# A hybrid encoder step on one core: in-place convolutions, spread row statistics, and queue positions for the next norm and the next mixer

## The chip, the cores and the metric

The kernel runs on one core of a Trainium2 chip. The metric is the device time of one execution in microseconds (us), as the median of several runs. A core has five engines that work side by side and meet only at semaphores: TensorE (PE) multiplies matrices out of SBUF into PSUM, VectorE (DVE), ScalarE (ACT) and GpSimd (POOL) work element by element, and SyncE (SP) here only issues DMA transfers. Each engine takes its instructions in one fixed order, so an instruction that waits holds everything queued behind it on the same engine. PSUM is small: a tile in it is free again only when the last instruction that reads it has ended.

## The reference

One step of one layer of a streaming encoder, in float32, over 1024 prompt tokens (one new stream) and 32 sample tokens (one running stream with carried states):

```python
h = mixer(rms_norm(x, g_mix_pre), ...)            # in-projection, three recurrences, out-projection
x = x + rms_norm(h, g_mix_post)
h = conv_ffn(rms_norm(x, g_ffn_pre), ...)         # up, causal convolution, gelu(gate)*val, down
x = x + rms_norm(h, g_ffn_post)
```

`mixer` projects each token's 1024 values with `w_in` to the inputs of three groups of heads:

- GLA, 6 heads (key width 32, value width 64): q, k, v, a low-rank gate that gives log-decays, and an output gate.
- HGRN2, 5 heads (64, 64): `q = silu(hq) / 8`, `k` and the log-decay from a sigmoid of one projection, and v.
- mLSTM, 5 heads (64, 64): q and k go through a causal convolution of width 4 and silu, and there are v, an input gate, a forget gate and an output gate. Its convolution's last three rows are returned as a cache, for the prompt and for the sample.

GLA and HGRN2 run S_t = diag(a_t) S_{t-1} + k_t v_t^T and o_t = S_t^T q_t; mLSTM runs a stabilised matrix memory with a running maximum m and a normaliser n. Each head's output is normalised (`x * rsqrt(mean(x*x) + 1e-6)`), multiplied by a gain and a gate, and the heads' outputs side by side (`cat`, 1024 wide) go through `w_out`. All final states are outputs.

## The kernel before

**Numbers and products.** A float32 product is made of three matmuls of the type fp32r: each operand is split into a high and a low part, and `mm3` (L99 to L102) adds high x high, high x low and low x high in PSUM. So each weight tile is loaded (`r`), its high part copied by ACT or DVE and its low part subtracted by POOL or DVE (`split`, L104 to L109). Group 0 stores the low parts to DRAM and groups 1 and 2 load them again (`weights`, `kept`).

**Groups.** The tokens come in units of 128 (u = 0 to 7; unit 8 is the 32 sample tokens) and the in-projection in three groups: units 0 to 2, units 3 to 5, and units 6, 7 and 8 (`GROUPS`, L27). For each group `inproj` (L352) is a generator whose steps are, in this order:

1. The norm. `scale_x` (L291) loads x of a unit, squares and sums it on ACT (L300), forms the reciprocal root on POOL (`rstd_of`, L216 to L219) and scales x on DVE (L303). `norm_group` (L306) turns the scaled x over on PE (xt, L314) and copies out high parts (ACT, xh L316) and low parts (DVE, xl L317). Between them the first token-major block, `vg(0)`.
2. Feature tiles, `feat(t)`: 128 output features by all tokens of the group, 24 matmuls each into one PSUM tile `pf` of the tag "big", which has three banks for everything that the projections make. Their order is 8 (a convolution), 6, 7, 3 (decays), 2, 0 (k and q of GLA), 4, 5, 1 (q of HGRN2, `silu_q` L529), 10 to 13 (convolutions). `silu_q` forms tanh(x/2) on ACT, scales it in place on DVE (L532: 0.0625 th + 0.0625) and multiplies it with the PSUM tile on DVE (L533); the factor 1/16 holds the 1/8 of the reference and the 1/2 of silu from tanh. `decay` and `decays` (L493 to L521) form the log-decays and their running sums. Results go to DRAM (`out_units`), where the mixer picks them up by unit.
3. A convolution, `conv(j, ps)` (L367 to L395): ACT copies the PSUM tile to `pc` (L372), POOL puts the three halo columns ahead and saves the new ones (L373, L374; `halo`), in group 2 the sample's columns and cache (`mcache`) go in and the caches are stored, two DMAs for each of five tiles (L378, L379). ACT forms y = pc * w3 + bias (L382), DVE adds three taps to y (L384), ACT takes its tanh, and DVE writes the product to a further tile `mo` (L389), which is stored. y has one buffer.
4. The mLSTM's row statistics, `rows()` (L541 to L600): running sums and maxima along five rows, then three tiny products of the decays (dcp, L590) copied to `dcs` (L592), and for each unit a transpose of the rows `r_st` (L596) copied to `cols` (L598). These small PSUM tiles come from a pool `psm` under a tag that the mixers use too (named mi in the profile). The generator is started after feature tile 3 and finished in one go after feature tile 1 (`next(row, None)`).
5. The token-major blocks 1 to 7 of 256 features: v and the output gates. `vg_store` (L408) copies v out on ACT (L412), or forms a gate from a tanh on ACT and one or two DVE operations. In group 2 `vg_across` makes them feature-major and turns them back (vf L456, pb L444). In block 5 of groups 0 and 1 the next group's `scale_x` is run. The loads of x for the next group are written there too.

**Mixers beside them.** `mixer(u, g, ci0)` (L700 to L965) is a generator for one unit, with two chunks of 64 tokens, in 17 steps. It loads `qkb` (q, k and the summed log-decays b; L703), mqk, v and gates in one step; forms eb = exp(b) on ACT (L743), dec and qz = q * eb on DVE; kh = exp(b_last - b) * k (DVE L758, ACT, DVE), turned over on PE and copied to kt (L767); six levels of decayed scores (sc, then P); the outputs og and oh and the states S (L857, L858); `finish` (L883 to L892: square on ACT, sum on DVE, reciprocal root, two products); then the mLSTM part with sm, kw, C, oi and om, and a last `finish`. `cat` goes to DRAM. The eight prompt mixers and the sample's one run beside what follows: those of group 0 beside the in-projection of group 1, and so on. `merge` (L1429) and `pump` take so many steps of the mixers for each step of the main generator. The last group's mixers run beside the out-projection, whose order of units is 0, 1, 2, 3, 8, 4, 5, then 6 and 7.

**Out-projection.** `outproj` (L994 to L1093) turns cat over (ctp, L1016), copies high and low halves out (ch L1019 on ACT, cl L1020 on DVE), multiplies with `w_out` (zp), squares and copies z, normalises it with the residual (L1060, L1061), forms the FFN's norm and turns it over for the FFN (fxt). The FFN, some half of the time, follows.

**What sets the order.** The program is written with a tile framework that puts the instructions of each engine in order by priority (the order in which the program issues them) along a simulated timeline. `tc.high_priority(offset=100)` moves instructions ahead by so many places; the small PE operations of the mixer go through it (`first`). `tc.issue_after(ins)` puts an instruction behind another one in the queue of the same engine.

Of the kernel before, what the change touches and what calls it, by code (L numbers as in the profile page):

```python
# [8 lines left out]
F32 = mybir.dt.float32  # L9
# [4 lines left out]
ALU = mybir.AluOpType  # L14
# [76 lines left out]
def body(ctx: ExitStack, tc: tile.TileContext, a: dict):  # L91
# [19 lines left out]
    def tanh(out, in_, scale):  # L111
        act.activation(out, in_, AF.Tanh, scale=scale)

# [101 lines left out]

    def rstd_of(out, ss, n, cols, width):  # L216

        pool.tensor_scalar(out, ss, 1.0 / width, EPS, op0=ALU.mult, op1=ALU.add)  # L218
        pool.tensor_tensor(out, out, mhalf[:n, :cols], op=ALU.pow)  # L219
# [68 lines left out]

    xn_of = {}

    def scale_x(g):  # L291
        for (u, off, n) in units_of(g):
            x = x_in.pop(u, None)
            x = load_x(u) if x is None else x
            if g == 0:
                jk = mx.tile([128, 1024], BF16, tag=("gt", "cat", "qkb")[u], name=f"jk{u}", bufs=1)
            else:
                jk = p1.tile([128, 1024], BF16, tag="jk", name=f"jk{u}", bufs=1)
            ss = p1.tile([128, 1], F32, tag="ss", name=f"ss{u}", bufs=2)
            act.activation(jk[:n], x[:n], AF.Square, accum_out=ss[:n])  # L300
            rs = p1.tile([128, 1], F32, tag="rs", name=f"rs{u}", bufs=2)
            rstd_of(rs[:n], ss[:n], n, 1, 1024)
            dve.scalar_tensor_tensor(x[:n], x[:n], rs[:n], gx[:n], op0=ALU.mult, op1=ALU.mult)  # L303
            xn_of[u] = x
            yield
# [46 lines left out]
    def inproj(g, xh, xl, normed, scaled=None):  # L352
# [16 lines left out]
        def conv(j, ps):  # L369
            W = 3 + pl + (3 + sl if sl else 0)  # L370
            pc = t1("pc", 2, W)
            act.copy(pc[:, 3:3 + pl], ps[:, :pl])  # L372
            pool.tensor_copy(pc[:, 0:3], halo[:, j, :])  # L373
            pool.tensor_copy(halo[:, j, :], pc[:, pl:pl + 3])  # L374
            if sl:
                act.copy(pc[:, pl + 6:pl + 6 + sl], ps[:, pl:T])
                pool.tensor_copy(pc[:, pl + 3:pl + 6], mcache[:, j, :])
                sp.dma_start(a["q_mc"][:, j, :], pc[:, W - 3:W])  # L378
                sp.dma_start(a["p_mc"][:, j, :], pc[:, pl:pl + 3])  # L379
            L = W - 3  # L380
            y = t1("y", 1, L)
            act.activation(y, pc[:, 3:], AF.Identity, scale=mconv[:, j, 3:4], bias=mconv[:, j, 4:5])  # L382
# [6 lines left out]
            ins = dve.scalar_tensor_tensor(o, th[:, :L], 1.0, y, op0=ALU.add, op1=ALU.mult)  # L389
            if j < 4:  # L390
                out_units(g, mqk_d, mqks_d, ((0, 1, 3, 4)[j], slice(None)), o, pl + 3)
            else:
                for slot, r0 in ((2, 0), (5, 64)):
                    out_units(g, mqk_d, mqks_d, (slot, slice(None)), o, pl + 3, slice(r0, r0 + 64), slice(0, 64))
            return ins  # L395
# [12 lines left out]
        def vg_store(blk, u, off, n, ps):  # L408
            o = mx.tile([128, 256], F32, tag="vg", name=f"vg{u}_{blk}", bufs=3)
            t = t0 + off  # L410
            if blk < 4:
                act.copy(o[:n], ps[:n, :256])  # L412
                sp.dma_start(v_d[t:t + n, 256 * blk:256 * blk + 256], o[:n])
                return
            c0 = 256 * (blk - 4)
            th = mx.tile([128, 256], F32, tag="vth", name=f"vth{u}_{blk}", bufs=1)
            tanh(th[:n], ps[:n, :256], 0.5)
            ns = min(max(704 - c0, 0), 256)
            if ns:
                dve.scalar_tensor_tensor(th[:n, :ns], th[:n, :ns], 1.0, ps[:n, :ns], op0=ALU.add, op1=ALU.mult)  # L420
            if ns < 256:
                dve.tensor_scalar(th[:n, ns:], th[:n, ns:], 1.0, None, op0=ALU.add)
            pool.tensor_tensor(o[:n], th[:n], gh[:n, c0:c0 + 256], op=ALU.mult)
            sp.dma_start(g_d[t:t + n, c0:c0 + 256], o[:n])
# [103 lines left out]

        def silu_q(q, ps, r0):  # L529
            th = t1("th", 1, T + 3)[:, :T]  # L530
            tanh(th[r0:], ps[r0:, :T], 0.5)
            dve.tensor_scalar(th[r0:], th[r0:], 0.0625, 0.0625, op0=ALU.mult, op1=ALU.add)  # L532
            return dve.tensor_tensor(q[r0:], th[r0:], ps[r0:, :T], op=ALU.mult)  # L533

# [6 lines left out]
        def rows():  # L541
# [51 lines left out]
            dcs_of[g] = dcs  # L593
            for (u, off, n) in units_of(g):
                pt = small(128)
                pe.transpose(pt[:n, :], st[:, off:off + n], ident)  # L596
                cl = mx.tile([128, 128], F32, tag="cols", name=f"cols{u}", bufs=6)
                act.copy(cl[:n], pt[:n])  # L598
                cols_of[u] = cl
# [81 lines left out]

    halves, kwi = [], [None]
    def spread(eng, dst, fn, n, half=None):
# [10 lines left out]
    def mixer(u, g, ci0):  # L694
# [47 lines left out]
        ebf = eb[:, :4 * n]  # L742
        act.activation(ebf, b4.rearrange("p f n -> p (f n)"), AF.Exp)  # L743
        eb4 = ebf.rearrange("p (f n) -> p f n", n=n)
# [3 lines left out]
        with ExitStack() as behind:  # L748
            if halves:

                for ins in (kwi[0], halves[1]):
# [5 lines left out]
        b5 = b4.rearrange("p f (k c) -> p (f k) c", c=cl)  # L757
        dve.tensor_tensor(khf.rearrange("p (m c) -> p m c", c=cl), b5[:, :, cl - 1:cl].broadcast_to([128, 4 * nch, cl]),  # L758
                          b5, op=ALU.subtract)
        act.activation(khf, khf, AF.Exp)  # L760
# [121 lines left out]

        def finish(o3, c0, h0, nh):  # L883
# [3 lines left out]
            act.activation(sq3, o3, AF.Square)  # L887
            dve.tensor_reduce(ss[:n, h0:h0 + nh], sq3, axis=mybir.AxisListType.X, op=ALU.add)  # L888
            rstd_of(rs[:n, h0:h0 + nh], ss[:n, h0:h0 + nh], n, nh, 64)
            dve.tensor_tensor(cat[:n, c0:c0 + 64 * nh].rearrange("p (h d) -> p h d", d=64), o3,  # L890
                              rs[:n, h0:h0 + nh].unsqueeze(2).broadcast_to([n, nh, 64]), op=ALU.mult)
            pool.tensor_tensor(cat[:n, c0:c0 + 64 * nh], cat[:n, c0:c0 + 64 * nh], gt[:n, c0:c0 + 64 * nh], op=ALU.mult)  # L892

        finish(og[:n], 0, 0, 6)
        finish(oh[:n], 384, 6, 5)

# [95 lines left out]
    def outproj(p2, W, u):  # L992
# [13 lines left out]
        for hf in range(2):  # L1006
# [7 lines left out]
            for k in range(4):  # L1014
# [3 lines left out]
            cl = p2.tile([128, 4, 128], F32R, tag="cl", name=f"cl{u}{hf}", bufs=3)  # L1018
            ins = (act.copy(ch[:, :, :n], ps[:, :, :n]),  # L1019
                   dve.tensor_tensor(cl[:, :, :n], ps[:, :, :n], ch[:, :, :n].bitcast(F32), op=ALU.subtract))  # L1020
            if u == RING[0]:
# [664 lines left out]
```

## Time and profile before

| | |
|---|---|
| runs | 1427.78, 1431.09 and 1431.6 us; median 1431.09 us |
| profiled execution | 1433.42 us, of which the trace's span is 1431.6 us |
| mean granted clock of PE | 0.983 |
| in-projection of group 0 | from the start to about 157 us |
| groups 1 and 2, with the mixers of the group before | to about 354 and 531 us |
| out-projection with the mixers of group 2 | to about 700 us |
| FFN | to the end |

The profile is one execution with each engine's instructions. Its page gives busy time by engine, the span in slices, the chain of work that ended last, and the costliest groups of instructions. The stage limits in the table are read from the timeline by the names of the tiles. The trace behind the page answers closer questions, and the prediction quotes four kinds of answer:

- Waits: engine, tile and line of the instruction that waited, what released it, and then total wait in us, number and longest.
- Stretches of time: limits and length, then busy us (and instructions) of PE, PE's weight loads, DVE, ACT and POOL, then the granted clock as a share of full speed, the DMA engines' mean busy share and GB/s.
- A timeline: start in us, duration in us, engine, line, operation, out<-in, shapes, and in brackets the idle time of the engine just before with what ended it.
- DMA groups: out<-in, queue, number, KB of one, and the median us from issue to landing.

### The profile page before, as it was taken

The page shows a single profiled execution, that of the slowest core. Times are in us where ns is not written, and L with a number is a line of the kernel's source. Part 1 is how long each engine was busy: PE and PEld are TensorE (multiplying, and loading weights), DVE is VectorE, ACT ScalarE, POOL GpSimd, SP SyncE. Part 2 cuts the span into 40 slices and gives each one's busy share as a digit, 9 for nine tenths or more (in the row PEclk, how much of TensorE's full clock was granted, in tenths as well). Part 3 has the DMA queues.
Part 4 walks back from the last instruction along what each step waited for, and adds up shares of the span by engine and source line. Part 5 has one row for each costly group of instructions (what it writes and reads, how often), then busy time and mean ns, then how long its engine had stood idle before and what let it go on. Part 6 is the DMA issues. An engine that isn't in the chain of part 4 may idle for free.

```text
span 1431.6 us, 30048 instructions
## 1 busy us (share of the span) xinstructions
PE 1375.1 (96%) x11804; PEld 1258.5 (88%) x11804; DVE 1006.9 (70%) x1827; ACT 710.2 (50%) x1403; POOL 273.5 (19%) x456
## 2 busy tenths in 40 slices
PE   7989999999998999899989999999999999999998
PEld 6989889898887887767789999999999999988886
DVE  5796468846597669685888887887888875653644
ACT  5545456535474546243665454554555455543432
POOL 6531111213021244132221111111111110000100
PEclk9999999999999999999999999999999999999999
DMA  9599778766789845352412222222222257775752
GB/s 345 189 317 355 229 244 298 236 228 210 262 248 303 313 124 188 122 178 60 162 54 91 85 82 91 75 78 73 91 75 75 76 183 235 227 230 180 238 180 99
DMA packets 132438, 255.11 MB, mean 178 GB/s; under 512 B 28648, under 2 KB 79368, under 8 KB 132296
## 3 DMA queue, kind: packets, MB, share of 16 engines
q1 hardware_dynamic: 132295, 253.19, 53.3%
q8 instruction: 92, 1.51, 0.4%
q14 instruction: 51, 0.41, 0.1%
HBM read 192.26 MB, written 60.89 MB: 177 GB/s over the span
## 4 chain that ended last, share of the span: by engine, by line
PE 71%; DVE 11%; DMA 8%; ACT 5%; issue 3%; POOL 2%; SPq 1%; DVEq 0%; POOLq 0%; ACTq 0%
PE pd L102 6%; PE pd L101 6%; PE pd L100 6%; PE pux L102 4%; PE pux L100 4%; PE pux L101 4%; PE pv L102 3%; PE pv L100 3%; PE pv L101 3%; PE puw L100 3%; PE puw L101 3%; PE puw L102 3%; DMA qkb<-qkb_d 2%; PE zp L100 2%; PE zp L101 2%
## 5 line engine op out<-in xcount | busy, mean ns | idle before, releaser
L1260 DVE SCALAR_TENSOR_TENSOR y<-uu,fconv_sb,y 128x1060 f32<-128x1060 f32 x88 | 116.3, 1321 | 28.3 <-ACT y L1258 27.5
L102 PE MATMUL pd<-wd,hl 128*128 128x512 f32 x264 | 105.1, 399 | 0.0
L101 PE MATMUL pd<-wd,hh 128*128 128x512 f32 x264 | 104.2, 395 | 0.0
L100 PE MATMUL pd<-wd,hh 128*128 128x512 f32 x264 | 103.5, 393 | 0.0
L1254 POOL COPY uu<-uu 128x2 f32<-128x2 f32 x44 | 35.3, 802 | 210.0 <-DVE uu L1202 209.9
L1197 ACT COPY c<-pux 128x274 f32<-128x274 f32 (+1 forms) x132 | 48.9, 375 | 41.2 <-PE pux L102 38.3
L1258 ACT ACTIVATE y<-uu,fconv_sb 128x1060 f32<-128x1060 f32 x44 | 56.0, 1273 | 21.1 <-POOL uu L1255 20.6
L100 PE MATMUL zp<-woh,ch 128*128 128x512 f32 (+1 forms) x144 | 58.8, 415 | 3.9 <-DVE cl L1020 2.9
L101 PEld LDWEIGHTS pd<-wd,hh 128*128 128x128 f32 x264 | 49.6, 188 | 12.5
L100 PEld LDWEIGHTS pd<-wd,hh 128*128 128x128 f32 x264 | 49.6, 188 | 11.7
L102 PEld LDWEIGHTS pd<-wd,hl 128*128 128x128 f32 x264 | 49.6, 188 | 11.4
L100 PE MATMUL pv<-wt_0h,xh 128*128 128x256 f32 (+2 forms) x195 | 57.8, 297 | 1.7 <-ACT xh L316 1.7
L101 PE MATMUL zp<-wol,ch 128*128 128x512 f32 (+1 forms) x144 | 58.8, 408 | 0.0
L102 PE MATMUL zp<-woh,cl 128*128 128x512 f32 (+1 forms) x144 | 58.2, 408 | 0.2 <-DVE cl L1020 0.2
L102 PE MATMUL pv<-wt_1h,xl 128*128 128x256 f32 (+2 forms) x195 | 57.4, 294 | 0.5 <-DVE xl L317 0.5
L102 PE MATMUL pv<-wt_0h,xl 128*128 128x256 f32 (+2 forms) x195 | 57.1, 293 | 0.6 <-DVE xl L317 0.6
L101 PE MATMUL pv<-wt_1l,xh 128*128 128x256 f32 (+2 forms) x195 | 56.9, 292 | 0.0
L100 PE MATMUL pv<-wt_1h,xh 128*128 128x256 f32 (+2 forms) x195 | 56.9, 292 | 0.0
L101 PE MATMUL pv<-wt_0l,xh 128*128 128x256 f32 (+2 forms) x195 | 56.8, 291 | 0.1
L100 PE MATMUL pd<-hh,wd 128*128 128x288 f32 x176 | 52.1, 297 | 0.0
L101 PE MATMUL pd<-hl,wd 128*128 128x288 f32 x176 | 52.1, 296 | 0.0
L218 POOL TENSOR_SCALAR hrs<-hss 128x5 f32<-128x5 f32 (+3 forms) x27 | 14.5, 537 | 196.4 <-DVE hss L888 195.8
(1675 smaller groups left out, 5179.5 us busy)
## 6 DMA issues: line engine op xcount, KB each, us to landing
h_d<-y SPq DMA_DIRECT2D x22, 530.0 KB, 3.3
wt_0r<-in_w_tok SPq DMA_DIRECT2D x21, 512.0 KB, 5.5
wt_1r<-in_w_tok SPq DMA_DIRECT2D x21, 512.0 KB, 5.9
wt_0l<-lt_d SPq DMA_DIRECT2D x14, 512.0 KB, 4.5
wt_1l<-lt_d SPq DMA_DIRECT2D x14, 512.0 KB, 5.6
qkb<-qkb_d SPq DMA_DIRECT2D x8, 768.0 KB, 6.4
hr<-h_d SPq DMA_DIRECT2D x44, 128.0 KB, 3.3
hr<-h_d SPq DMA_DIRECT2D x22, 192.0 KB, 4.1
```

Of the source, the lines that this page charges most:

```text
L100: pe.matmul(ps, lh[0], rh[0], start=first, stop=False, **kw)
L101: pe.matmul(ps, lh[0], rh[1], start=False, stop=False, **kw)
L102: return pe.matmul(ps, lh[1], rh[0], start=False, stop=last, **kw)
L218: pool.tensor_scalar(out, ss, 1.0 / width, EPS, op0=ALU.mult, op1=ALU.add)
L1197: kept[name] = act.copy(t, ps)
L1254: pool.tensor_copy(u[:, GAP_P:GAP_P + 2], u[:, GAP_S - 2:GAP_S])
L1258: act.activation(y, u, AF.Identity, scale=fconv[:, j, 2:3], bias=fconv[:, j, 3:4])
L1260: dve.scalar_tensor_tensor(y, uu[i][:, s:s + NCOL], fconv[:, j, s:s + 1], y, op0=ALU.mult, op1=ALU.add)
```

## The change

It touches the in-projections, the mixers' beginnings and two copies of the out-projection. No matmul is added or removed, and the FFN is as it was.

1. `silu_q` is one DVE operation, (th + 1) * ps. HGRN2's q is thereby 16 times larger; `finish` for its heads takes 16 * 16 * 1e-6 in place of 1e-6 (`by=16.0`), so that the norm gives the same.
2. `conv` works in place: y has three buffers, the product is written to y, and `mo` is gone. In group 2 the caches are gathered in `mcache` and `halo` (one more small POOL copy for each of five tiles) and stored once, two DMAs in place of ten.
3. `rows()` gives up control before the small products and before each transpose, and is taken up after each of the four last convolution tiles. In group 0 the transposes go to a PSUM tile of their own (`rows0`, under the tag "o").
4. `scale_x` of groups 1 and 2: the square is put behind ACT's last tanh of `vg_store` and the scaling behind DVE's last gate operation (`vgi`). The loads of x are issued in block 2.
5. `mixer`: qkb is loaded in two DMAs, b first. The exponential eb is put behind the previous mixer's second square of `finish` on ACT, and kh's subtraction behind the previous mixer's last addition to S on DVE (`outs`).
6. `outproj`: the copies ch and cl are issued at a priority 100 places ahead.

```diff
@@ scale_x
-            act.activation(jk[:n], x[:n], AF.Square, accum_out=ss[:n])
+            with tc.issue_after(vgi[0].ins) if vgi else ExitStack():
+                act.activation(jk[:n], x[:n], AF.Square, accum_out=ss[:n])
             rs = p1.tile([128, 1], F32, tag="rs", name=f"rs{u}", bufs=2)
             rstd_of(rs[:n], ss[:n], n, 1, 1024)
-            dve.scalar_tensor_tensor(x[:n], x[:n], rs[:n], gx[:n], op0=ALU.mult, op1=ALU.mult)
+            with tc.issue_after(vgi[1].ins) if vgi else ExitStack():
+                dve.scalar_tensor_tensor(x[:n], x[:n], rs[:n], gx[:n], op0=ALU.mult, op1=ALU.mult)
@@ conv
-                sp.dma_start(a["q_mc"][:, j, :], pc[:, W - 3:W])
-                sp.dma_start(a["p_mc"][:, j, :], pc[:, pl:pl + 3])
+                pool.tensor_copy(mcache[:, j, :], pc[:, W - 3:W])
+                if j == 3:
+                    sp.dma_start(a["q_mc"], mcache)
+                    sp.dma_start(a["p_mc"], halo)
             L = W - 3
-            y = t1("y", 1, L)
+            y = t1("y", 3, L)
...
-            o = t1("mo", 2, L)
-            ins = dve.scalar_tensor_tensor(o, th[:, :L], 1.0, y, op0=ALU.add, op1=ALU.mult)
+            ins = dve.scalar_tensor_tensor(y, th[:, :L], 1.0, y, op0=ALU.add, op1=ALU.mult)
...
@@ vg_store
-            tanh(th[:n], ps[:n, :256], 0.5)
+            ia = tanh(th[:n], ps[:n, :256], 0.5)
...
+            vgi[:] = ia, iv
@@ silu_q
-            dve.tensor_scalar(th[r0:], th[r0:], 0.0625, 0.0625, op0=ALU.mult, op1=ALU.add)
-            return dve.tensor_tensor(q[r0:], th[r0:], ps[r0:, :T], op=ALU.mult)
+            return dve.scalar_tensor_tensor(q[r0:], th[r0:], 1.0, ps[r0:, :T], op0=ALU.add, op1=ALU.mult)
@@ rows
             yield
+
+            own = psm.tile([128, 3, 128], F32, tag="o", name="rows0", bufs=2) if g == 0 else None
             dcp = small(3, 8)
...
-            for (u, off, n) in units_of(g):
-                pt = small(128)
+            for i, (u, off, n) in enumerate(units_of(g)):
+                yield
+                pt = small(128) if own is None else own[:, i]
                 pe.transpose(pt[:n, :], st[:, off:off + n], ident)
@@ inproj
         decays(2, ins)
-
-        next(row, None)
         yield
         for t, j in ((10, 0), (11, 1), (12, 2), (13, 3)):
             ins = conv(j, feat(t))
             if j == 0:
                 decays(3, ins)
+
+            next(row, None)
             yield
...
             yield from vg(blk)
+            if blk == 2 and g < 2:
+                for (u, off, n) in units_of(g + 1):
+                    x_in[u] = load_x(u)
@@ mixer
-        sp.dma_start(qkb[:, :12 * n], (qkb_d[u] if u < 8 else qkbs_d).rearrange("p a f n -> p (a f n)"))
+        for s0, s1 in ((2, 3), (0, 2)):
+            sp.dma_start(qkb[:, 4 * n * s0:4 * n * s1],
+                         (qkb_d[u] if u < 8 else qkbs_d)[:, s0:s1].rearrange("p a f n -> p (a f n)"))
...
-        act.activation(ebf, b4.rearrange("p f n -> p (f n)"), AF.Exp)
+        with tc.issue_after(outs[0].ins) if outs else ExitStack():
+            act.activation(ebf, b4.rearrange("p f n -> p (f n)"), AF.Exp)
...
+        with tc.issue_after(outs[1].ins) if outs else ExitStack():
+            dve.tensor_tensor(khf.rearrange("p (m c) -> p m c", c=cl), b5[:, :, cl - 1:cl].broadcast_to([128, 4 * nch, cl]),
+                              b5, op=ALU.subtract)
...
-            dve.tensor_tensor(Sn, Sn, up, op=ALU.add)
+            si = dve.tensor_tensor(Sn, Sn, up, op=ALU.add)
...
+        outs[:] = finish(oh[:n], 384, 6, 5, 16.0), si
@@ outproj
-            ins = (act.copy(ch[:, :, :n], ps[:, :, :n]),
-                   dve.tensor_tensor(cl[:, :, :n], ps[:, :, :n], ch[:, :, :n].bitcast(F32), op=ALU.subtract))
+            with tc.high_priority(offset=AHEAD):
+                ins = (act.copy(ch[:, :, :n], ps[:, :, :n]),
+                       dve.tensor_tensor(cl[:, :, :n], ps[:, :, :n], ch[:, :, :n].bitcast(F32), op=ALU.subtract))
```

More of the change, by code (lines that the diff above doesn't have):

```diff
@@ L111, in tanh @@
     def tanh(out, in_, scale):
-        act.activation(out, in_, AF.Tanh, scale=scale)
+        return act.activation(out, in_, AF.Tanh, scale=scale)
     dr = ctx.enter_context(tc.tile_pool(name="dr", bufs=1, space=DRAM))
@@ L214, in body, with rstd_of @@
     dve.tensor_scalar(oml, lb, -1.0, 1.0, op0=ALU.mult, op1=ALU.add)
-    def rstd_of(out, ss, n, cols, width):
-        pool.tensor_scalar(out, ss, 1.0 / width, EPS, op0=ALU.mult, op1=ALU.add)
+    def rstd_of(out, ss, n, cols, width, eps=EPS):
+        pool.tensor_scalar(out, ss, 1.0 / width, eps, op0=ALU.mult, op1=ALU.add)
         pool.tensor_tensor(out, out, mhalf[:n, :cols], op=ALU.pow)
@@ L287, in norm_tiles @@
                 p1.tile([128, 8, T], F32R, tag="xl", name=f"xl{g}"))
-    xn_of = {}
+    xn_of, vgi = {}, []
     def scale_x(g):
@@ L387, in conv @@
             tanh(th[:, :L], y, (1.0, 1.0, 8.0, 8.0, tsc)[j])
-            o = t1("mo", 2, L)
-            ins = dve.scalar_tensor_tensor(o, th[:, :L], 1.0, y, op0=ALU.add, op1=ALU.mult)
+            ins = dve.scalar_tensor_tensor(y, th[:, :L], 1.0, y, op0=ALU.add, op1=ALU.mult)
             if j < 4:
-                out_units(g, mqk_d, mqks_d, ((0, 1, 3, 4)[j], slice(None)), o, pl + 3)
+                out_units(g, mqk_d, mqks_d, ((0, 1, 3, 4)[j], slice(None)), y, pl + 3)
             else:
                 for slot, r0 in ((2, 0), (5, 64)):
-                    out_units(g, mqk_d, mqks_d, (slot, slice(None)), o, pl + 3, slice(r0, r0 + 64), slice(0, 64))
+                    out_units(g, mqk_d, mqks_d, (slot, slice(None)), y, pl + 3, slice(r0, r0 + 64), slice(0, 64))
             return ins
@@ L680, in body @@
     state = {}
-    halves, kwi = [], [None]
+    halves, kwi, outs = [], [None], []
     def spread(eng, dst, fn, n, half=None):
@@ L881, in mixer, with finish @@
         rs = mx.tile([128, 16], F32, tag="hrs", name=f"hrs{u}", bufs=2)
-        def finish(o3, c0, h0, nh):
+        def finish(o3, c0, h0, nh, by=1.0):
             sq = mx.tile([128, 384], F32, tag="sq", name=f"sq{u}_{h0}", bufs=1)
             sq3 = sq[:n, :64 * nh].rearrange("p (h d) -> p h d", d=64)
-            act.activation(sq3, o3, AF.Square)
+            sqi = act.activation(sq3, o3, AF.Square)
             dve.tensor_reduce(ss[:n, h0:h0 + nh], sq3, axis=mybir.AxisListType.X, op=ALU.add)
-            rstd_of(rs[:n, h0:h0 + nh], ss[:n, h0:h0 + nh], n, nh, 64)
+            rstd_of(rs[:n, h0:h0 + nh], ss[:n, h0:h0 + nh], n, nh, 64, EPS * by * by)
             dve.tensor_tensor(cat[:n, c0:c0 + 64 * nh].rearrange("p (h d) -> p h d", d=64), o3,
@@ L892, in finish @@
             pool.tensor_tensor(cat[:n, c0:c0 + 64 * nh], cat[:n, c0:c0 + 64 * nh], gt[:n, c0:c0 + 64 * nh], op=ALU.mult)
+            return sqi
         finish(og[:n], 0, 0, 6)
-        finish(oh[:n], 384, 6, 5)
+        outs[:] = finish(oh[:n], 384, 6, 5, 16.0), si
         yield
```

6 lines of the change are left out of this document (2 added, 4 removed).

## The prediction

> **What bounds the kernel now.** I read the first part of the page, then stretches of the span with the busy time of each engine, then the list of what TensorE (PE) waited for.
>
> ```profile
> span 1431.6 us, 30048 instructions
> PE 1375.1 (96%) x11804; PEld 1258.5 (88%) x11804; DVE 1006.9 (70%) x1827; ACT 710.2 (50%) x1403; POOL 273.5 (19%) x456
> ```
>
> ```profile
> 25.00:700.00 675.00, 642.61 (x6678) 567.24 (x6677) 468.83 (x1019) 337.98 (x716) 166.01 (x216) 0.97 0.70 230
> 750.00:1431.60 681.60, 675.17 (x4751) 638.54 (x4749) 479.75 (x728) 325.13 (x603) 77.43 (x195) 1.00 0.39 130
> ```
>
> PE is the bound: 1375.1 of 1431.6 us. The second row is the FFN; PE rests in it 6.4 us, nearly all at the end, and the change leaves it alone. The first row holds all three in-projections, the mixers beside them and the out-projection. There PE rests 675.0 - 642.6 = 32.4 us, and the granted clock averages 0.97. The change takes no matmul away (the 18 small products of the row statistics are only moved), so it can win no more than those 32 us and the time lost to a lower clock.
>
> PE's waits, with total, count and longest:
>
> ```profile
> PE pf L100 <- DVE q L533: 3.4, 1, 3.4
> PE pb L444 <- ACT vf L456: 3.3, 1, 3.3
> PE zp L100 <- DVE cl L1020: 2.9, 3, 2.5
> ...
> PE mi L692 <- ACT kt L767: 2.6, 2, 2.1
> ...
> PE xt L314 <- ACT vg L412: 1.8, 1, 1.8
> ...
> PE mi L596 <- ACT dcs L592: 1.3, 1, 1.3
> PE sm L692 <- DVE cat L890: 1.2, 1, 1.2
> ...
> PE pv L102 <- DVE xl L317: 1.0, 4, 0.5
> PE mi L596 <- ACT cols L598: 1.0, 1, 1.0
> ```
>
> And stretches with the clock in the last column but two:
>
> ```profile
> 70.80:73.20 2.40, 0.79 (x7) 0.69 (x6) 1.10 (x1) 1.27 (x2) 1.45 (x1) 1.00 0.85 184
> 73.20:80.00 6.80, 5.05 (x16) 5.05 (x17) 6.66 (x8) 1.44 (x2) 3.84 (x2) 0.50 1.03 350
> 172.20:175.60 3.40, 3.40 (x21) 2.95 (x19) 2.24 (x4) 1.31 (x5) 0.56 (x2) 0.50 0.02 5
> ...
> 421.40:424.70 3.30, 3.30 (x16) 3.30 (x15) 3.21 (x9) 2.34 (x7) 0.00 (x0) 0.50 0.96 244
> 462.30:465.70 3.40, 3.40 (x15) 3.01 (x14) 3.32 (x9) 1.08 (x4) 0.94 (x2) 0.50 1.03 417
> ...
> 575.00:581.70 6.70, 5.82 (x14) 4.60 (x15) 4.49 (x10) 1.15 (x2) 0.74 (x2) 0.50 0.67 203
> ```
>
> Each of the five stretches at 0.50 lies around or just behind one wait (their times come below: q, xt, r_dc, vf, cl). Half of such a stretch is lost: 3.4, 1.7, 1.65, 1.7 and 3.35 us.
>
> **The change part by part.**
>
> *The gated q of HGRN2 (L532, L533).* In group 0 this stands around the 3.4 us wait, on POOL and on DVE:
>
> ```profile
> 71.75 2.34 POOL L109 TENSOR_TENSOR wf_11l<-wf_11r,wf_11h 128x1024 fp32r<-128x1024 f32 x1 [4.36 <-ACT wf_11h L106]
> ```
>
> ```profile
> 72.10 2.21 DVE L532 TENSOR_SCALAR th<-th 128x384 f32<-128x384 f32 x1 [2.20 <-ACT th L112]
> 74.34 0.56 DVE L533 TENSOR_TENSOR q<-th,pf 128x384 f32<-128x384 f32 x1
> ```
>
> And, earlier in the group, a DVE pass beside a POOL pass:
>
> ```profile
> 23.61 0.69 DVE L317 TENSOR_TENSOR xl<-xt,xh 128x512 fp32r<-128x512 f32 x1 [0.83 <-ACT xh L316]
> ```
>
> ```profile
> 22.74 2.37 POOL L109 TENSOR_TENSOR wf_8l<-wf_8r,wf_8h 128x1024 fp32r<-128x1024 f32 x1 [1.28 <-ACT wf_8h L106]
> ```
>
> The scaling took 2.21 us and ended just after POOL's pass (74.09): the two did not run side by side. PE needed the PSUM bank that q frees at 74.90. One instruction with an SBUF and a PSUM operand takes the place of both. Its price is 0.56 us (L533) or, if POOL held it up too, 2.2. I take 0.56, since L317, with one operand in PSUM, took its usual 0.69 beside a POOL pass. The bank is then free at 72.7: 2.2 us earlier. Six small products (L590), six of the seven matmuls that made 0.79 us in 70.8 to 73.2, move out of this gap and cost PE their 0.7 us elsewhere: -2.2 + 0.7 = -1.5. PE still rests 3.4 - 1.5 = 1.9 us here; behind a rest of that length (r_dc, below) a stretch of 3.3 us stands, so of the clock loss only 3.4 - 1.7 = 1.7 goes. In groups 1 and 2 the saving lies beside PE's work.
>
> *Row statistics.* Group 0 gets a bank of its own for its transposes, so the waits for dcs and cols go: 1.3 + 1.0 = -2.3. In group 2 PE waited for r_dc:
>
> ```profile
> 419.21 0.27 PE L590 MATMUL mi<-r_dc,cf_sb 5*128 5x5 f32 x1 [1.86 <-ACT r_dc L577]
> ```
>
> These products move behind the 24 matmuls of the next feature tile. From 421.4 sixteen such matmuls filled 3.3 us at half speed, so 24 take 2.5 at full, longer than r_dc was late: -1.9, clock -1.65. The mixer that reads these columns begins only after the group, so spreading costs nothing there.
>
> *Convolutions in place.* y has three buffers and no copy mo.
>
> ```profile
> 256.43 0.71 ACT L382 ACTIVATE y<-pc,mconv_sb 128x384 f32<-128x384 f32 x1 [1.97 <-DVE mo L389]
> ...
> 257.48 0.74 ACT L767 COPY kt<-mi 64x256 f32<-64x256 f32 x2
> ```
>
> ACT stood 1.97 us because the only y was still read; behind it in the queue stood kt, for which PE waited 2.1. With a second y this wait goes: -2.1. The caches go out in 2 stores instead of 10, for 5 tiny POOL copies; both lie on engines that are not late here, and cost nothing unless POOL were the one awaited.
>
> *Next norm behind the evictions.*
>
> ```profile
> 167.84 1.06 ACT L300 ACTIVATE jk<-x 128x1024 bf16<-128x1024 f32 x1 [4.23 <-DMA x<-in_xp]
> ...
> 169.09 0.38 ACT L412 COPY vg<-pv 128x256 f32<-128x256 f32 x1
> ```
>
> This square belongs to group 2 but sits in group 1's first block: ACT waited 4.23 us for x and the eviction of pv stood behind it. Held back to block 5, it cannot do that: -1.8, clock -1.7. Squares and scalings now fall into blocks 5 to 7; the transposes xt of the next group wait for them, on PE. Their cover is the two blocks that follow. An xl that DVE gave late cost PE at most 0.5, so three scalings may cost 3 x 0.5: +1.5. Nothing at all, and three whole waits like xt's (5.4), are the ends.
>
> *Next mixer's decays behind the finish.*
>
> ```profile
> 456.99 0.63 ACT L743 ACTIVATE eb<-qkb 128x512 f32<-128x512 f32 x1 [7.91 <-DMA qkb<-qkb_d]
> ...
> 461.14 0.68 ACT L456 COPY vf<-pv 128x288 f32<-128x288 f32 x2
> ```
>
> ACT stood 7.91 us before eb, with vf behind it; PE lost 3.3 waiting for vf. Now eb queues behind the previous mixer's second square and kh behind its last state sum: -3.3, clock -1.7. What waits longer for eb and kh are dec, qz and kt, needed only after six levels. The load of qkb becomes two, b first.
>
> ```profile
> qkb<-qkb_d SPq DMA_DIRECT2D x8, 768.0 KB, 6.4
> ...
> hr<-h_d SPq DMA_DIRECT2D x22, 192.0 KB, 4.1
> ...
> mqk<-mqk_d SPq DMA_DIRECT2D x16, 128.0 KB, 6.2
> ```
>
> A third of the size lands in 4.1 to 6.2 us by the nearest rows, so the split alone wins between 0.2 and 2.3 us on a path that is no longer PE's; I count nothing, and nothing for the second issue on SP.
>
> *Halves of cat ahead (L1019, L1020).*
>
> ```profile
> 573.26 1.87 DVE L1060 SCALAR_TENSOR_TENSOR z<-z,oss,gm 128x1024 f32<-128x1024 f32 x1 [0.52 <-POOL oss L219]
> 575.06 0.68 DVE L1020 TENSOR_TENSOR cl<-ctp,ch 128x512 fp32r<-128x512 f32 x1
> ```
>
> The low half came behind a wide DVE pass and 0.52 us of rest. Ahead of both it runs from 572.74 to 573.4, and PE asked at 575.74 - 2.5 = 573.2: -2.5 less 0.2, clock -3.35.
>
> *The rule of the clock.* The rows show half speed behind rests of 1.8 and 1.9 us (xt, r_dc). [...]
>
> *Sum.* Waits: 1.5 + 2.3 + 1.9 + 2.1 + 1.8 + 3.3 + 2.3 = 15.2. Clock: 1.7 + 1.65 + 1.7 + 1.7 + 3.35 = 10.1. Against it I set three estimates: behind each of the five waits after group 0 PE meets the next short one of a mixer sooner, like sm's 1.2 us, 5 x 1.2 = 6.0; of the clock gains half comes back, 5.05; and the scalings, 1.5. So 25.3 - 12.55 = 12.75 us less. The profiled execution took 1433.4 us, 2.3 above the median of the runs (1431.1), so the median becomes about 1418.
>
> **The rivals.**
>
> *The waits change their name.* In 462.3 to 465.7 the DMA share is 1.03 and ACT has work. If weights and evictions are late anyway, only group 0's terms stay, 1.5 + 1.7 + 2.3 = 5.5, less the 1.5 of the scalings: 1427. For it: the DMA share. Against: average DMA share is 0.70.
>
> *The last mixers come late.* The forced order delays eb if the square stays where it is:
>
> ```profile
> 547.22 0.63 ACT L743 ACTIVATE eb<-qkb 128x512 f32<-128x512 f32 x1 [2.32 <-DMA qkb<-qkb_d]
> ...
> 553.41 0.42 ACT L887 ACTIVATE sq<-oh 32x320 f32<-32x320 f32 x1
> ...
> 599.53 0.64 ACT L743 ACTIVATE eb<-qkb 128x512 f32<-128x512 f32 x1 [5.74 <-DMA qkb<-qkb_d]
> ...
> 609.22 0.42 ACT L887 ACTIVATE sq<-oh 128x320 f32<-128x320 f32 x1
> ```
>
> That is 6.2 us for the mixer of unit 6 and 9.7 for unit 7, whose output the last out-projection needs. If both reach PE, 15.9 us plus two half-speed stretches of 3.4 (3.4 lost) make 19.3 against the 12.75: 1437 or 1438. It decides where more than 12.75 us of this reach PE. Against: the squares were themselves late behind the new mixer's work, and PE has other units' matmuls meanwhile.
>
> *Everything holds.* No short wait grows and the clock stays up: 25.3 less, 1406.
>
> [...]
>
> That the change does not do what it says would show as eb ahead of sq again; the first rival prices it.
>
> **How the numbers follow.** Forecast 0.52 (1412 to 1425). Names change 0.22 (1425 to 1434; 0.05 of it faster, 0.15 same, 0.02 slower). Late mixers 0.14. Everything holds 0.06. Clock rule 0.06. A measurement of this kernel can tell about 0.3%, 4.3 us. Faster: 0.52 + 0.06 + 0.06 + 0.05 = 0.69; same 0.15; slower 0.14 + 0.02 = 0.16. From 1407 to 1434 leaves out the late mixers and part of the best case.
>
> **What would show it.** Right: no wait of PE on q L533's line, on dcs, r_dc, or kt behind y; group 2's squares behind group 1's block 5 and not at 168; eb behind sq in every mixer; clock 1.00 in most of 150 to 470. Wrong: new PE waits over 2 us on xt or on oi and om in the out-projection, or the rest of PE from 25 to 700 us still near 32.

## The result, and the profile after

| | median | runs |
|---|---|---|
| before | 1429.35 us | 12, from 1427.35 to 1434.54 |
| after | 1422.55 us | 12, from 1416.82 to 1428.06 |

The ratio is 0.9947, with a 95% interval from 0.993 to 0.9963: 6.8 us less. The forecast was 1418, in a range from 1407 to 1434; of the 12.75 us that it took off, about half came. The profiled execution of after took 1421.18 us, 12.2 less than that of before. Of that, 5.4 us are only how far these two executions lie from the medians of their kernels.

The page of after:

```profile
span 1419.4 us, 30029 instructions
...
PE 1368.0 (96%) x11804; PEld 1253.1 (88%) x11804; DVE 1009.2 (71%) x1818; ACT 711.3 (50%) x1403; POOL 281.9 (20%) x461
```

The stretches that were read before (limits and length, then busy PE, PEld, DVE, ACT, POOL, clock, DMA share, GB/s):

```profile
25.00:700.00 675.00, 645.47 (x6739) 571.07 (x6737) 483.04 (x1022) 347.14 (x730) 177.78 (x230) 0.97 0.69 232
750.00:1419.00 669.00, 662.86 (x4651) 626.12 (x4649) 470.00 (x712) 320.58 (x590) 75.45 (x191) 1.00 0.37 131
```

In 25 to 700 us PE rests 675.0 - 645.5 = 29.5 us, where it rested 32.4 before, and the clock is 0.97 as before. The FFN is the same. A fixed stretch holds more work in the kernel that is ahead, so the same place in the work is the better mark. From the start to the 61st matmul of `puy`, at the beginning of the FFN, in before and then in after (length, then busy time by engine):

```profile
sum 764.60, PE 714.53 PEld 634.56 DVE 539.25 ACT 392.70 POOL 199.18; mean PE 178.63 PEld 158.64 DVE 134.81 ACT 98.17 POOL 49.80
```

```profile
sum 753.00, PE 708.11 PEld 630.03 DVE 540.74 ACT 393.38 POOL 207.08; mean PE 177.03 PEld 157.51 DVE 135.19 ACT 98.35 POOL 51.77
```

PE rests 44.9 us instead of 50.1, and its busy time is 6.4 us less with about as many matmuls. So 5.2 us of rest went, where the sum counted 15.2 of waits: the change removed waits, and others came in their place. Rows of PE's waits of after say which:

```profile
...
PE pv L100 <- ACT xh L318: 5.4, 4, 2.5
PE zp L100 <- DVE z L1105: 5.2, 3, 2.9
PE rows L603 <- ACT cols L605: 2.7, 1, 2.7
...
PE om L702 <- DVE w L927: 2.3, 1, 2.3
PE pf L100 <- DVE q L537: 1.9, 1, 1.9
PE mi L596 <- ACT kt L781: 1.6, 1, 1.6
```

Of the waits shown before, those for dcs and r_dc and of xt behind vg are gone, vf, cl and cat are down to 0.2, 0.2 and 0.3 us, kt to 1.6, and q's fell from 3.4 to 1.9. In their places stand xh (1.7 before), z (1.0), cols (1.0) and w (0.4), the mLSTM weights that the product om needs.

### The profile page after: what moved, and what is told of

Same layout as the page of the kernel before. It is cut to its first block, busy times and chain, and to the rows that moved or that the text cites. A ratio compares the mean times of both kernels' runs of the same rounds, so it can differ in the third digit from the quotient of the medians.

```text
span 1419.4 us, 30029 instructions
## 1 busy us (share of the span) xinstructions
PE 1368.0 (96%) x11804; PEld 1253.1 (88%) x11804; DVE 1009.2 (71%) x1818; ACT 711.3 (50%) x1403; POOL 281.9 (20%) x461
## 4 chain that ended last, share of the span: by engine, by line
PE 78%; DVE 8%; DMA 5%; ACT 4%; issue 2%; POOL 2%; SPq 1%; DVEq 0%; POOLq 0%; ACTq 0%
PE pd L102 6%; PE pd L101 6%; PE pd L100 6%; PE pux L100 4%; PE pux L102 4%; PE pux L101 4%; PE pv L100 3%; PE pv L102 3%; PE pv L101 3%; PE puw L101 3%; PE puw L100 3%; PE puw L102 3%; PE zp L100 2%; PE pf L100 2%; PE pf L101 2%; PE zp L101 2%
## 5 line engine op out<-in xcount | busy, mean ns | idle before, releaser
L100 PE MATMUL pd<-hh,wd 128*128 128x288 f32 x176 | 52.0, 296 | 0.0
L102 PE MATMUL pd<-hh,wd 128*128 128x288 f32 x176 | 51.8, 296 | 0.0
```

The source lines that it names most:

```text
L100: pe.matmul(ps, lh[0], rh[0], start=first, stop=False, **kw)
L102: return pe.matmul(ps, lh[1], rh[0], start=False, stop=last, **kw)
```

## The experiments

Two theories were tried. The first is the prediction's: the parts add up, and each gives about half of its own waits. The rival gives the whole gain to one part. First it was tried with the mixers' queue order, and when that fell, with the gated q. Each part was put alone on the kernel before, some parts were taken out of the change, and two were altered. All ratios are to the kernel before on the same chip, with 95% intervals.

| kernel | what it has | median us | ratio |
|---|---|---|---|
| e_q | gated q alone | 1422.8 | 0.9951 (0.9938 to 0.9963) |
| e_rowsq | gated q and row statistics | 1419.93 | 0.9928 (0.9906 to 0.9949) |
| b_banks | the same, a PSUM tile for each transpose | 1422.24 | 0.9941 (0.9919 to 0.9963) |
| e_norm | next norm alone | 1431.21 | 1.0008 (0.9993 to 1.0022) |
| e_conv | convolutions alone | 1432.33 | 1.0012 (0.9994 to 1.003) |
| e_order | eb and kh queued behind, alone | 1430.36 | 0.9998 (0.9986 to 1.001) |
| e_split | qkb in two loads, alone | 1431.62 | 1.001 (0.9994 to 1.0026) |
| e_mixer | these two together | 1440.79 | 1.0068 (1.0049 to 1.0086) |
| e_halves | ch and cl ahead, alone | 1429.93 | 0.9997 (0.9985 to 1.0009) |
| u_mixer | the change without the mixer's part | 1420.6 | 0.9931 (0.991 to 0.9952) |
| a_nosplit | the change with qkb in one load | 1421.61 | 0.9939 (0.9918 to 0.9961) |
| a_late_free | the change, last three mixers not queued | 1421.38 | 0.9931 (0.9914 to 0.9947) |

All kernels with the new q lie between 1419.9 and 1422.8 us, whatever else they have; all with the old q lie at 1429.9 or above. The change without the new q was not run. The medians of the kernel before in these comparisons were 1429.5 to 1431.2.

**Gated q and row statistics (e_rowsq), gated q alone (e_q).** The first has the diff's edits to `silu_q`, `finish` and `rows`, the second only this and the 16 in `finish`:

```diff
-            dve.tensor_scalar(th[r0:], th[r0:], 0.0625, 0.0625, op0=ALU.mult, op1=ALU.add)
-            return dve.tensor_tensor(q[r0:], th[r0:], ps[r0:, :T], op=ALU.mult)
+            return dve.scalar_tensor_tensor(q[r0:], th[r0:], 1.0, ps[r0:, :T], op0=ALU.add, op1=ALU.mult)
```

> Before with the changed gated q and the changed row statistics alone. Theory (the parts add up, each gives about half of its own waits): PE's wait for q's bank is 1.9 us instead of 3.4 and the wait for dcs is gone; a wait for cols of 2 to 3 us stands in group 0, because its three transposes share one PSUM tile, as in the trace of the change; the wait before the r_dc products in group 2 stays at 1 to 2 us, for a PSUM bank. Time 1 to 3 us below before. Rival (the mixers' queue order carries the whole gain): time within 1 us of before.

> Before with the gated q of HGRN2 as one operation, alone. Theory (the wait of group 0 and its half-speed stretch are its worth): PE's wait for q's bank is 1.9 us or less, time 2 to 4 us below before. Rival (one DVE pass less for nine tiles, three of them in each group, carries the 10 us of q and row statistics together): 8 to 10 below before, with the gain spread over groups 1 and 2.

e_rowsq came out 10 us below before, far more than the theory's 1 to 3, and e_q 6.7 below, between its theory and its rival; e_q's gain lies in groups 0 and 1, not 2. Neither has the mixers' queue order, so that order carries nothing of this. PE's wait for q is 1.9 us in e_rowsq. In e_q, where the six small products still fill a part of the gap, it is 1.1, and the one for dcs is 2.7 (1.3 in before, 2.2 in e_halves):

```profile
PE mi L596 <- ACT dcs L592: 2.7, 1, 2.7
...
PE pf L100 <- DVE q L533: 1.1, 1, 1.1
```

The expected wait of 1 to 2 us before the r_dc products of group 2 is not in e_rowsq. Its group 2 takes 178.4 us, against 182.3 in e_q (below):

```profile
342.70:521.10 178.40, 169.34 (x2210) 150.94 (x2208) 123.29 (x333) 96.50 (x226) 37.95 (x55) 0.98 0.77 254
```

That is near the 3.55 us that the sum gave this term. But the intervals of e_rowsq and e_q overlap, and b_banks, which has the row statistics too, is at 1422.24 us: they add nothing that is certain.

Where e_q wins is best read against e_halves, which is nearly the kernel before run again: the order of instructions is that of before on DVE, ACT, POOL and SyncE over the whole span, and on PE up to the out-projection but for one small matmul. The stretches of groups 0, 1 and 2 in e_halves, then in e_q:

```profile
0.00:157.30 157.30, 139.25 (x944) 133.79 (x945) 106.18 (x156) 80.33 (x144) 63.05 (x66) 0.98 0.87 300
157.30:350.00 192.70, 188.23 (x2179) 171.81 (x2177) 133.93 (x314) 101.17 (x204) 38.28 (x55) 0.98 0.72 242
350.00:532.40 182.40, 171.80 (x2208) 153.75 (x2207) 123.75 (x336) 96.28 (x226) 39.43 (x55) 0.96 0.75 249
```

```profile
0.00:155.20 155.20, 138.47 (x943) 132.77 (x944) 104.03 (x153) 80.69 (x144) 62.45 (x66) 0.99 0.87 303
155.20:341.60 186.40, 183.94 (x2179) 167.89 (x2178) 132.57 (x311) 100.77 (x204) 38.05 (x55) 1.00 0.75 251
341.60:523.90 182.30, 172.29 (x2210) 153.13 (x2208) 123.53 (x334) 96.34 (x226) 37.61 (x55) 0.96 0.74 249
```

Group 0 is 2.1 us shorter, group 1 is 6.3 us shorter, group 2 is the same. In group 1 PE rests 186.4 - 183.9 = 2.5 us instead of 4.5, and the clock is 1.00 instead of 0.98. In e_halves PE waits there 2.05 us for kt until 255.6, where a half-speed stretch of 6.83 us begins, which costs 3.4; in e_q neither is there: 2.05 + 3.4 of these two traces' 6.3 us. But e_conv, with the old q, has no wait for kt there either, and its group 1 takes 192.4 us, so this wait is not the cause by itself.

That the gain belongs to the new q and not to one execution, the other traces show. Seven kernels have the old q and seven the new one, with one trace each. Group 0 takes 156.7 to 159.3 us in the seven with the old q and 153.8 to 156.1 in the others; group 1 takes 189.6 to 196.8 us and 186.4 to 188.2. In group 1 the middle values are 192.4 and 187.8, so 4.6 us is the fairer size. PE rests 3.2 to 6.9 us there with the old q and 2.5 to 4.0 with the new one, and stands 3.4 to 13.7 us at half speed against 0 to 3.4. How the shorter q brings this about, three DVE passes fewer in the group, is not shown; the scheduler also placed other instructions differently.

**Next norm (e_norm)** and **convolutions (e_conv)**, as in the diff.

> Before with the next norm queued behind the gates, and its loads in block 2, alone. Theory (the parts add up): the square of group 2 leaves group 1's first block, PE's wait for xt behind ACT's vg (1.8 us) is gone, the first pv of groups 1 and 2 waits no more than 1 us for xh; time 1 to 3 us below before. Rival (the mixers' queue order carries the whole gain): within 1 us of before, since a wait for xh of 2 to 3 us at a group's beginning takes the place of the one for xt.

> Before with the in-place convolutions and the caches stored once, alone. Theory (the parts add up): PE's wait for kt (2.1 us at 258) is gone and the mixers of group 1's stage end 1 to 2 us earlier; time 1 to 2 us below before. Rival (the mixers' queue order carries the whole gain): within 1 us of before.

Neither is faster. The theory's 1 to 3 and 1 to 2 us are outside the intervals or at their very ends (a gain of 1.0 us for e_norm, 0.9 for e_conv), and the rival's 0 is inside. Their traces show what came instead. Rows of PE's waits of e_norm, then of e_conv:

```profile
...
PE pv L100 <- ACT xh L318: 4.7, 4, 1.9
...
PE pb L447 <- ACT vf L459: 3.3, 1, 3.3
```

```profile
PE sc L693 <- DVE Qz L818: 3.8, 2, 3.1
```

In e_norm the wait of xt behind vg is gone, as the theory has it, and the first pv of group 1 waits 1.9 us for xh instead of 0.4. In e_conv the wait for kt at 258 us is gone, and in group 2, where PE waited 3.3 us for vf until 461.6, it waits 3.1 us for Qz until 456.6.

**The mixer's part (e_mixer), and its halves (e_order, e_split).** e_mixer has both of these edits, e_order the second (for kh likewise), e_split the first:

```diff
-        sp.dma_start(qkb[:, :12 * n], (qkb_d[u] if u < 8 else qkbs_d).rearrange("p a f n -> p (a f n)"))
+        for s0, s1 in ((2, 3), (0, 2)):
+            sp.dma_start(qkb[:, 4 * n * s0:4 * n * s1],
+                         (qkb_d[u] if u < 8 else qkbs_d)[:, s0:s1].rearrange("p a f n -> p (a f n)"))
...
-        act.activation(ebf, b4.rearrange("p f n -> p (f n)"), AF.Exp)
+        with tc.issue_after(outs[0].ins) if outs else ExitStack():
+            act.activation(ebf, b4.rearrange("p f n -> p (f n)"), AF.Exp)
```

> Before with the mixer's part alone: qkb in two loads, eb and kh queued behind the previous mixer's last square and last state sum. Theory (the parts add up): PE's wait for pb behind vf (3.3 us) is gone; time 2 to 4 us below before. Rival (the mixers' queue order carries the whole gain): 6 to 8 us below before, as the whole change.

> Before with eb and kh queued behind the previous mixer's last square and last state sum, qkb still in one load. Theory (the forced order costs the 10 us of the mixer's part): 7 to 12 us above before. Rival (the second load, in the queue of DMA issues ahead of the weights, costs them): within 3 us of before.

> Before with qkb loaded in two DMAs, b first, alone. Theory (the second load moves the weights' loads back in the queue of DMA issues): 6 to 12 us above before, with a wait of PE for the low half of a weight tile in group 2 and SyncE's waits ahead of the weights' loads (lt_d) over 25 us instead of 19. Rival (only load and forced order together cost the 10 us): within 3 us of before.

Both theories fall with e_mixer: it is 10 us slower, and neither half alone costs or gains anything that can be measured. Rows of PE's waits in e_mixer, in e_order and in e_split:

```profile
PE sm L692 <- DVE cat L894: 2.9, 1, 2.9
PE pv L102 <- DMA wt_1l<-lt_d: 2.7, 1, 2.7
```

```profile
PE sm L692 <- DVE cat L892: 2.1, 1, 2.1
```

```profile
PE mi L692 <- DVE S L860: 4.6, 1, 4.6
```

The wait for vf is down to 0.6 us in e_mixer and off the list in the others, and in the same place in group 2 PE waits 2.1 to 4.6 us for cat or S. Group 2 in e_mixer is its slow part:

```profile
348.90:541.00 192.10, 179.63 (x2197) 159.79 (x2196) 126.66 (x336) 96.53 (x226) 38.07 (x55) 0.94 0.72 235
```

It takes 192.1 us at a clock of 0.94; e_order takes 185.1 there and e_split 185.7, both at 0.96. PE's wait of 2.7 us for the low half of a weight tile is not in e_split; in e_order it is 1.6 us. SyncE stood 29.2 us before these loads in e_mixer and 19.1 before, but also 27.0 in e_order, which is no slower. Half-speed stretches fill 24.0 us of group 2 in e_mixer and 13.8 and 14.1 in the two halves; half of the excess, 5 us, is lost time. Why only the pair costs 10 us was not settled.

**The change without it (u_mixer), with one load (a_nosplit).** Edits as above, taken back.

> The change without the mixer's part (qkb in one load, eb and kh not put behind anything). Theory (the parts add up, and the mixer's part costs about 10 us in the whole change as it did alone): 8 to 12 us below the change, so 15 to 19 below before. Rival (the mixer's part costs only where the other parts are missing): within 3 us of the change.

> The change with qkb in one load; eb and kh still queued behind the previous mixer. Theory (the second load costs in the whole change too): 4 to 10 us below the change. Rival (its cost depends on where the weights' loads stand, and the other parts have moved them): within 3 us of the change.

Both rivals hold: 2 us and 1 us below the change, which the intervals do not tell from nothing. What costs 10 us on the kernel before costs nothing that can be measured where the other parts have moved the work around it.

**Halves of cat ahead (e_halves).** The edit of `outproj` alone.

> Before with the copies ch and cl of the out-projection 100 places ahead, alone. Theory (the parts add up: -10 for q and rows, 0 for norm and convolutions, +10 for the mixer, so about -7 is left for this part): 5 to 9 us below before, all of it in the out-projection. Rival (the parts do not add up, and this one only exchanges the wait for cl for one for z): within 2 us of before.

The rival holds by the time, but for another reason than it gives. A row of PE's waits of e_halves:

```profile
PE zp L100 <- DVE cl L1021: 3.1, 3, 2.7
```

and DVE in front of that wait:

```profile
568.46 1.87 DVE L1061 SCALAR_TENSOR_TENSOR z<-z,oss,gm 128x1024 f32<-128x1024 f32 x1 [0.72 <-POOL oss L219]
570.26 0.68 DVE L1021 TENSOR_TENSOR cl<-ctp,ch 128x512 fp32r<-128x512 f32 x1
```

The low half still comes behind the wide pass, 1.87 us long, that waits for POOL, as it did before. A priority is a wish to the scheduler; here it left the order of DVE and ACT as it was, and moved only a few matmuls on PE. So this run does not tell what copies that run ahead would be worth.

**Banks for the transposes (b_banks).** e_rowsq with

```diff
-            own = psm.tile([128, 3, 128], F32, tag="o", name="rows0", bufs=2) if g == 0 else None
...
-                pt = small(128) if own is None else own[:, i]
+                pt = small(128) if g else psm.tile([128, 128], F32, tag="o", name=f"rows{u}", bufs=2)
```

> Before with the gated q as one operation and the spread row statistics, where each of group 0's three transposes has a PSUM tile of its own instead of a third of one. Theory (the wait of 2.7 us for cols is only the shared tile): that wait is gone or under 1 us, group 0 ends 1 to 2.7 us earlier than with the shared tile, and the time is 10 to 13 us below before. Rival (ACT's copies are late anyway and the next matmuls wait for a bank of pf instead): group 0 ends where it ended with the shared tile.

The wait for cols in group 0 is gone, so it was the shared tile. The time is 7.7 us below before, not 10 to 13, and no better than with the shared tile, as the rival has it. Group 0 takes 154.1 us and took 154.6. In it stands a wait at 114 us that was not there before:

```profile
PE pv L100 <- ACT vg L412: 1.7, 1, 1.7
```

It also has a half-speed stretch of 3.41 us at 73.5, 1.7 us lost, which e_rowsq has not, so the two traces alone do not tell what the tile is worth.

**The last mixers free (a_late_free).** The change with `if outs and g < 2` in both places where eb and kh are put behind, so that units 8, 6 and 7 are not.

> The change with eb and kh put behind the previous mixer only in the mixers of the first six units; those that run beside the out-projection (units 8, 6, 7) are free, as before. Theory (the forced order wins in group 2's in-projection and costs about 4 us in the out-projection): group 2 takes 176 to 179 us as in the change, the stretch from the first zp to the FFN's third up tile 227 to 229 us instead of 232, PE's wait for om behind w (2.3 us) is gone, and the time is 2 to 5 us below the change. Rival (the out-projection's length varies with the half-speed stretches of one execution and not with the order): the wait for om stays or is replaced by one as long, and the time is within 1 us of the change.

The rival holds by the time, and group 2 takes 182.0 us, not the theory's 176 to 179. The wait of om for w is gone, waits for w (1.3 us, at oi) and for cl (2.6 us) stand in its place, and the stretch from the first zp to the 61st matmul of puy takes 232.9 us, as in the change (232.0). PE rests less in it, 14.1 us instead of 17.8, but 30.2 us of it run at half speed instead of 18.1, so one trace cannot tell what the free order is worth there. 1421.38 against 1422.55 us is within 0.3%. No version beats the change by more than the measurement can tell.

## Why the prediction was right in its range and wrong in its parts

**The total came near by luck.** Of the 12.75 us the sum gave 3.2 to q and 9.55, after its three allowances, to the five other parts. By the medians q won 6.7, and the others nothing that can be measured. The two errors, 3.5 us too little and about 9.5 too much, have opposite signs, and the range is 27 us wide.

**The bound held.** PE is the bound, the FFN did not move, and what could be won lay in the rests and the clock of 25 to 700 us. But two signs that were named for being wrong did come: om in the out-projection waits 2.3 us for w, and PE's rest from 25 to 700 us is 29.5, near 32.

**The gated q was priced right as an instruction and too small as a term.** DVE and POOL of after around that wait:

```profile
72.20 0.55 DVE L537 SCALAR_TENSOR_TENSOR q<-th,pf 128x384 f32<-128x384 f32 x1 [2.20 <-ACT th L112]
72.67 1.98 DVE L515 SCALAR_TENSOR_TENSOR e<-fr,e 128x384 f32<-128x384 f32 x1
```

```profile
71.86 2.38 POOL L109 TENSOR_TENSOR wf_11l<-wf_11r,wf_11h 128x1024 fp32r<-128x1024 f32 x1 [4.36 <-ACT wf_11h L106]
```

With one operand in PSUM the instruction takes 0.55 us in the middle of POOL's pass; the next one, with all its tensors in SBUF, takes 1.98 and ends at 74.65, just behind POOL's end at 74.24. In before the same instruction took 0.55 us, at 74.81, when POOL's pass was over. PE's wait became the forecast 1.9 us. The failed step is "In groups 1 and 2 the saving lies beside PE's work": in group 1 alone e_q wins 6.3 us against e_halves, and 4.6 by the middle values of seven traces each. The term was 3.2 us in the sum and is 6.7 us by the medians, all that the whole change measures.

**The other terms were not independent.** The prediction added 15.2 us of waits from seven places and took off 6.0 for the next short waits. The runs show more: one wait can be removed by several edits, and the next one takes most of what it was worth. The wait for kt at 258 us goes in e_conv alone and in e_q alone; vf's 3.3 us in group 2 is 3.1 for Qz in e_conv, 2.1 for cat in e_order, 3.6 for S in e_q. The first rival (the waits change their name, 1427) described this and held for the parts behind group 0. It had q too small, and it counted 2.3 us for dcs and cols, where the wait only moved.

**Row statistics.** "The waits for dcs and cols go" failed: dcs went, and cols rose from 1.0 to 2.7 us, because the own bank was one tile that PE could not write while ACT had yet to read it. "Longer than r_dc was late" held for r_dc, but in the change 1.6 us of the wait stayed, now for kt, which held the PSUM tile that the small products need; in e_rowsq none stayed.

**Norm.** The estimate of 1.5 us for three scalings was too small: the four waits of pv for xh grew from 1.7 to 5.4 us, +3.7, which is more than the 1.8 that went.

**Mixer.** eb runs behind the square, at 446.52 after 446.20 in the change, as forecast, and vf's wait is gone. What was won was not measurable. The rival of the late mixers (19 us) did not come, but for om's 2.3 us.

**Halves.** "Ahead of both it runs" failed outright in e_halves. In the change cl's wait went, and one of 2.9 us for z stands there. That hangs on the forced order of the last mixers: in u_mixer and a_late_free, which have this part without that order, PE waits 2.5 and 2.6 us for cl again.

**The clock terms came from one execution.** 10.1 us were read off the half-speed stretches of one trace. Group 1 in before took as follows; in e_halves, with the same instructions, it took 192.7 us (above).

```profile
157.00:353.80 196.80, 189.95 (x2179) 173.09 (x2178) 133.88 (x314) 100.55 (x204) 38.19 (x55) 0.97 0.71 237
```

In the one, PE waits 1.8 us for xt, and half-speed stretches stand at 172 and 291 us; in the other it waits 0.3 us for xt, and one stands at 255. Six traces with the old q put group 1 between 189.6 and 193.0, and only that of before at 196.8. So about 4 us of the profiled pair's 12.2 were never the change's to win. The stretch at 291 is in no other trace. The one at 172, which the sum priced at 1.7 us, stands between 169 and 173 us in e_conv, e_mixer, e_order and e_split too, but not in e_halves.

## What to carry to other kernels

Where one engine is busy nearly all the time and its rests are a dozen short waits, removing a wait is worth what comes late next, not its length: test each part alone before its price is added to others. Shortening what a nearly bound engine's helper does won more here (6.7 us by the medians) than putting instructions in another order, which alone won nothing that could be measured: one DVE pass took the place of two, and with an operand in PSUM it took 0.55 us in the middle of POOL's pass of 2.38, where the scaling that went had taken 2.21 beside such a pass. A stretch at half speed should be priced only if it is there in more than one execution. And an experiment on the order of instructions should first show that the order changed.

## What the runs showed of the hardware

The stretches at half clock are 3.41 us long or two, three or four times that (6.83 and 10.24 us in before, 13.65 in the change), but for the last, which the end of the trace cuts. Within a trace they begin at whole multiples of 3.413 us from each other; in the change, for example, at 92.02, 160.29 and 348.02 us, 20 and 55 of them apart. Whether a wait is followed by one depends on more than its length. The old q's wait of 3.36 to 3.40 us has a stretch around or behind it in all seven traces that hold it; the new q's wait of 1.87 to 1.91 us in three of six; a wait of 2.71 to 2.74 us, wherever it stands, in four of seven. The plainest pair is the wait for cols in group 0 of the change and of a_late_free, whose instructions are the same there. In both PE rested 2.72 us until 90.60 us after the start. The rest and what followed, in the change and then in a_late_free:

```profile
87.90:90.60 2.70, 0.00 (x0) 0.00 (x0) 2.63 (x5) 1.25 (x5) 0.98 (x2) 1.00 1.05 375
92.10:95.40 3.30, 3.30 (x12) 3.30 (x11) 3.24 (x6) 2.12 (x5) 0.50 (x1) 0.50 1.02 382
```

```profile
87.90:90.60 2.70, 0.00 (x0) 0.00 (x1) 2.63 (x5) 1.25 (x5) 0.99 (x2) 1.00 1.05 370
92.10:95.40 3.30, 3.30 (x25) 3.30 (x24) 3.24 (x6) 2.13 (x5) 0.50 (x1) 1.00 1.03 389
```

Twelve matmuls against 25 in the same 3.3 us.

What differs is where the rest falls. Cut each trace into windows of 3.413 us at the places where its stretches begin. In the change a limit lies at 88.61 us, so 1.99 us of the rest fall into one window; in a_late_free it lies at 89.10, and the rest is split into 1.22 and 1.50. The 14 traces, from 12 to 1400 us, agree. Of the windows at full speed in which PE rested 1.8 us or more, 45 of 46 were followed by one at half speed; from 1.0 to 1.8 us, 57 of 140; below 1.0, 20 of 3088, and 14 of these 20 are one place just ahead of the out-projection, once in each trace. So rest is not all that counts, but it fits q: a wait of 3.36 us puts at least 1.68 us into one window wherever it falls. The new q's wait lay whole in one window in the three traces with a stretch, and was split, with at most 1.49 us in one, in the three without.

So the sum's rule that each of these short waits costs a stretch fell: the new q's waits of 1.9 us had one in three of six traces. Whether one had a stretch went, in these 14 traces, with where the windows of its execution lay.
